# Indexer scores over four PSUM banks, and a retention chunk's two head pairs in one bank each for products, states and outputs

## The chip, the cores and the metric

The kernel runs on one core of one Trainium2 chip. The metric is the device time of one launch in microseconds (us). TensorE (PE in the profile) multiplies, VectorE (DVE), ScalarE (ACT) and GpSimd (POOL) work on its results, SyncE (SP) issues the transfers. PSUM, into which TensorE writes, has eight banks of 128 partitions by 512 floats.

## What is computed

Two decoder layers over 1024 positions of width 1024. Each layer norms the input, projects it, and runs three branches whose gated outputs are merged: retention (chunks of 128 positions with a recurrent state), a sparse attention whose indexer picks 256 keys for each query, and a gated linear attention (GLA). Cut to what the change touches:

```
def dsa_attention(q, k, v, q_idx, k_idx, w_idx, pos):        # blocks of 128 queries
        s = jnp.einsum('bqhd,bsd->bqhs', qib, k_idx_f) * (IDX_DH ** -0.5)     # 4 indexer heads
        score = jnp.einsum('bqh,bqhs->bqs', wb, jax.nn.relu(s))
        score = jnp.where(visible[None], score, -jnp.inf)
        _, sel = lax.top_k(score, topk)                                       # topk = 256
def retention(q, k, v, pos):                                  # 8 chunks of 128, 4 heads
    scores = jnp.einsum('bnihd,bnjhd->bnhij', qc, kc) * decay
    o_intra = jnp.einsum('bnhij,bnjhe->bnihe', scores, vc)
    kv = jnp.einsum('bnjhd,bnjhe->bnhde', kc * to_end[None, None, :, :, None], vc)
    state -> chunk_decay * state + kv_n
    o_cross = jnp.einsum('bnihd,bnhde->bnihe', q_dec, prev)
    return (o_intra + o_cross)
```

## The kernel before

Each layer begins with the indexer. `idx_proj` projects eight blocks of 128 positions, and `idx_scores` does blocks 2 to 7: for each piece of up to 512 keys and each of four heads TensorE makes the head's scores with two matmuls (lines 500 and 501, from a high and a low part of the keys), ScalarE takes the positive part into a buffer `tr` (line 503, three buffers), and VectorE adds it, weighted, into the block's score row `mk` (lines 506 and 509). That makes 40 heads of a piece in a layer. A head uses one PSUM bank of the tag `sc`, of which there are two.

The top-k of the sparse attention (`topk`, lines 854 and 855) works on those rows. A step is a search for the eight largest values (MAX8) and their replacement (a small load, then MATCH_REPLACE8), each over the whole row; a block takes 32 steps. Blocks 2 to 5 may run as soon as their rows stand, and they fill VectorE between its other work.

Retention follows. `ret_v` makes the values (eight groups of 24 matmuls over the shared helper lines 223 to 225, into the banks `acc`), `ret_qk` makes queries and keys of a chunk (another such group), turns them on VectorE (lines 540 to 544, the rotation; only the last of the three, line 544, gives the `acc` bank back) and transposes them. `ret_scan` does the recurrence of chunk p, one pair of heads after the other: the products of queries and keys (line 572, bank `sc`), their decay on VectorE into `at` (line 574), the carried part (line 577, bank `o`), the new state's product (line 580, bank `sc`), the state's update on VectorE (line 585), the decayed products with the values (line 590, the same bank `o`), and on ScalarE the sums of squares (line 594) and the copy out of `o` (line 595). The gate's groups (`ret_gate`, 24 matmuls a chunk; line 613 gives their bank back) and GLA's projections come next.

The eight banks have owners: `acc` 1, `tp` 2, `o` 1, `sc` 2, and two spare ones, `x` and `y`, that a table lends out. During the indexer and retention both are lent to `acc`:

```
    own = {"acc": 1, "tp": 2, "o": 1, "sc": 2}
    spare = {"x": "acc", "y": "acc"}
        extra = [e for e in sorted(spare) if spare[e] == tag]
        n = turn[tag] = (turn[tag] + 1) % (own[tag] + len(extra))
```

No order is written by hand. The program is built with a scheduler (`schedule_with_timeline_sim=True`) that sets each engine's order ahead of time; on the chip every engine then runs its list in that order and waits at each instruction for what it needs. TensorE's matmuls of `ret_v`, `ret_qk` and the gates, called the fill below, are what the scheduler puts between the small steps of scores and scan.

Of the kernel before, what the change touches and what calls it, by code (L numbers as in the profile page):

```python
# [10 lines left out]
FT = mybir.dt.float32  # L11
# [5 lines left out]
OP = mybir.AluOpType  # L17
# [56 lines left out]
def tile_trunk(ctx: ExitStack, tc: tile.TileContext, x, c, positions, ada_w, ada_b, pre_norm, post_norm,  # L74
# [17 lines left out]
    def pool(name, bufs=1, side=None):  # L92
        return tc.alloc_tile_pool(name=name, bufs=bufs, side=side, reuse_waits="tile")
# [18 lines left out]
    def otp():  # L112
        return bank("o")

    def scp():
        return bank("sc")
# [127 lines left out]
    def blk(p):  # L244
        return slice(p * 128, (p + 1) * 128)
# [206 lines left out]
    for l in range(depth):  # L452
# [40 lines left out]
        def idx_scores(i):  # L493
            w = mk[i]
            N = (i + 1) * 128
            for c0 in range(0, N, 512):
                n = min(512, N - c0)
                for h in range(4):
                    ps = scp()
                    T.matmul(ps[:, :n], qst[:, i - 2, h], ksh[:, c0:c0 + n], start=True, stop=False)  # L500
                    T.matmul(ps[:, :n], qst[:, i - 2, h], ksl[:, c0:c0 + n], start=False, stop=True)
                    r = pi_.tile([128, 512], FT, tag="tr", bufs=3, name="tr")
                    A.activation(r[:, :n], ps[:, :n], AF.Relu)
                    wh = wts[:, i, h:h + 1]
                    if h:
# [3 lines left out]
                        V.tensor_scalar(w[:, c0:c0 + n], r[:, :n], wh, None, op0=OP.mult)  # L509
            V.tensor_add(w[:, N - 128:N], w[:, N - 128:N], cau_inv)  # L510

        for p in range(NB):
            idx_proj(p)
        for i in range(2, NB):
# [50 lines left out]

        def ret_scan(p, got):
            qz, kT, qd, kd = got
            for g in range(2):
                gs = slice(g * 256, (g + 1) * 256)
                old, new = sts[g][(p + 1) % 2], sts[g][p % 2]  # L570
                sp = scp()[:, 0:256]
                T.matmul(sp, kT[:, g], qz[:, g].rearrange("p s n -> p (s n)"), start=True, stop=True)
                at = prb.tile([128, 256], FT, tag="at", bufs=2, name="at")
                V.tensor_mul(at, sp, kc[:, K_DEC + g * 256:K_DEC + (g + 1) * 256])
                op = otp()[:, 0:256]
                if p:
                    T.matmul(op, qd[:, g], old, start=True, stop=False)
                if p < NB - 1:
                    kv = scp()[:, 0:256]
                    T.matmul(kv, kd[:, 2 * g:2 * g + 2].rearrange("p h d -> p (h d)"), vo[:, p, gs],  # L580
                             start=True, stop=True)
                    for s in range(2):
                        rs = slice(s * 64, (s + 1) * 64)
                        if p:
                            V.scalar_tensor_tensor(new[rs, blk(s)], old[rs, blk(s)], kc[rs, K_CD + g:K_CD + g + 1],
                                                   kv[rs, blk(s)], op0=OP.mult, op1=OP.add)
                        else:
                            V.tensor_copy(new[rs, blk(s)], kv[rs, blk(s)])
                for s in range(2):
                    T.matmul(op[:, blk(s)], at[:, blk(s)], vo[:, p, blk(2 * g + s)], start=p == 0,  # L590
                             stop=p == 0 or s == 1)
                sq = prb.tile([128, 128], BF, tag="sq", bufs=1, name="sq")
                for s in range(2):
                    A.activation(sq, op[:, blk(s)], AF.Square, accum_out=ssq[:, p, 2 * g + s:2 * g + s + 1])
                A.copy(vo[:, p, gs], op)
            rsq(rr[:, p, :], ssq[:, p, :], 4, 4.0 / 128, 4 * EPS)

        def head_gate(pl, wg, p, o2, r2, dst):
# [28 lines left out]
        for p in range(NB):  # L627
# [2 lines left out]
                ret_scan(p - 1, held)  # L630
            held = got
        ret_scan(NB - 1, held)
        br = pool(f"brr{l}", side="right")
        brh = br.tile([128, 4, S], FR, name="brh")
        brl = br.tile([128, 4, S], FR, name="brl")
# [480 lines left out]
```

## Time and profile before

| | |
|---|---|
| median of 3 runs | 2487.65 us (2483.64 to 2490.65) |
| the profiled execution | 2489.89 us |
| its span, first to last instruction | 2488.1 us |
| PE busy | 2395.1 us, 96% of the span |
| DVE busy | 1704.3 us, 68% |
| ACT, POOL busy | 892.9 us, 915.0 us |
| indexer's first score, layer 0 and layer 1 | 101.63 us, 1316.47 us |

Busy time is the sum over an engine's instructions. The profile also tells the TensorE clock that was granted in a stretch, as a share of full speed (1.00 is 2.4 GHz, half of it 1.2 GHz), and at a wait the instruction that ended it.

### The profile page before, as it was taken

How to read it: one execution, taken by the hardware profiler on the slowest of the kernel's cores; microseconds unless marked ns; L12 is line 12 of the kernel's file. 1: busy time of each engine (PE TensorE's matmuls, PEld its weight loads, DVE VectorE, ACT ScalarE, POOL GpSimd, SP SyncE). 2: the span in 40 equal slices, each digit the busy share in tenths (PEclk: the TensorE clock that was granted, in tenths of full speed). 3: DMA queues.
4: the chain of work that ended last, by engine and by line, in shares of the span. 5: the costliest groups of instructions: out<-in, count | busy, mean ns of one | idle time of the engine just before them, and what ended most of it. 6: DMA issues, size and time to landing. Idle time of an engine off the chain costs nothing.

```text
span 2488.1 us, 38048 instructions
## 1 busy us (share of the span) xinstructions
PE 2395.1 (96%) x13680; PEld 2032.5 (82%) x13680; DVE 1704.3 (68%) x3513; ACT 892.9 (36%) x2147; POOL 915.0 (37%) x1304
## 2 busy tenths in 40 slices
PE   8898999999999999999999899999999999999998
PEld 4777788888878998887788677887898789888777
DVE  6599997348749964567567999933554899356652
ACT  4333432232321236663433234222333212566421
POOL 4324344534522352106641244443454225310350
PEclk9999999999999999999999899999999999999999
DMA  8011112224412212007620111222321221210453
GB/s 273 22 35 35 35 41 79 59 87 145 119 60 76 66 48 64 27 22 246 201 90 1 35 35 48 64 61 85 85 63 41 85 85 35 71 41 22 140 199 110
DMA packets 153115, 194.95 MB, mean 78 GB/s; under 512 B 18703, under 2 KB 109147, under 8 KB 152926
## 3 DMA queue, kind: packets, MB, share of 16 engines
q1 hardware_dynamic: 152926, 192.52, 25.4%
q8 instruction: 107, 1.75, 0.3%
q14 instruction: 82, 0.67, 0.1%
HBM read 154.71 MB, written 37.77 MB: 77 GB/s over the span
## 4 chain that ended last, share of the span: by engine, by line
PE 73%; DVE 15%; DMA 4%; issue 3%; POOL 3%; ACT 2%; SPq 0%; DVEq 0%; POOLq 0%; ACTq 0%
PE acc L223 18%; PE acc L224 18%; PE acc L225 18%; DVE mk L855 3%; PE tp L936 2%; DVE m L854 2%; DMA craw<-in_ada_w 2%; PE sc L762 2%; PE o L958 1%; PE sc L921 1%; PE o L955 1%; PE sc L922 1%; PE o L962 1%; PE sc L223 1%; PE sc L224 1%
## 5 line engine op out<-in xcount | busy, mean ns | idle before, releaser
L223 PE MATMUL acc<-whi,hTh 128*128 128x256 f32 (+1 forms) x1600 | 509.8, 319 | 15.5 <-DVE rb L544 8.0
L225 PE MATMUL acc<-whi,hTl 128*128 128x256 f32 (+1 forms) x1600 | 507.4, 317 | 0.0
L224 PE MATMUL acc<-wlo,hTh 128*128 128x256 f32 (+1 forms) x1600 | 506.9, 317 | 0.0
L177 POOL TENSOR_TENSOR wlo<-raw,whi 128x512 fp32r<-128x512 f32 x216 | 283.1, 1318 | 374.8 <-ACT whi L176 343.6
L223 PE MATMUL acc<-hTh,whi 128*128 128x512 f32 x896 | 355.4, 397 | 2.7 <-ACT mt L287 1.8
L224 PE MATMUL acc<-hTl,whi 128*128 128x512 f32 x896 | 353.3, 394 | 0.0
L225 PE MATMUL acc<-hTh,wlo 128*128 128x512 f32 x896 | 352.7, 394 | 0.0
L854 DVE MAX8 m<-mk 128x8 f32<-128x512 f32 (+5 forms) x384 | 341.7, 892 | 8.2
L223 PEld LDWEIGHTS acc<-whi,hTh 128*128 128x128 f32 x1600 | 307.1, 192 | 41.3 <-issue 11.7
L855 DVE MATCH_REPLACE8 mk<-m,mk 128x512 f32<-128x512 f32 (+5 forms) x384 | 336.6, 877 | 0.2
L225 PEld LDWEIGHTS acc<-whi,hTl 128*128 128x128 f32 x1600 | 306.8, 192 | 20.0 <-issue 2.4
L224 PEld LDWEIGHTS acc<-wlo,hTh 128*128 128x128 f32 x1600 | 307.0, 192 | 19.0 <-issue 2.2
L176 ACT CAST whi<-raw 128x512 fp32r<-128x512 f32 x216 | 133.8, 622 | 217.9 <-PE acc L224 139.0
L223 PEld LDWEIGHTS acc<-hTh,whi 128*128 128x128 f32 x896 | 169.0, 189 | 39.9 <-ACT mt L287 2.8
L225 PEld LDWEIGHTS acc<-hTh,wlo 128*128 128x128 f32 x896 | 169.0, 189 | 37.1 <-issue 2.4
L224 PEld LDWEIGHTS acc<-hTl,whi 128*128 128x128 f32 x896 | 169.1, 189 | 34.1 <-issue 1.9
L940 DVE TENSOR_TENSOR ptl<-tp,pth 128x512 fp32r<-128x512 f32 (+1 forms) x160 | 100.6, 635 | 68.6 <-ACT pth L939 59.3
L287 ACT ACTIVATE mt<-acc 128x512 f32<-128x512 f32 x96 | 57.2, 599 | 191.1 <-PE acc L225 136.3
L218 POOL TENSOR_TENSOR wlo<-raw,whi 128x512 fp32r<-128x512 f32 x56 | 76.7, 1378 | 111.2 <-ACT whi L217 110.4
L926 ACT ACTIVATE P<-P,mx 128x256 f32<-128x256 f32 (+7 forms) x128 | 99.8, 781 | 47.0 <-DVE mx L923 46.1
L939 ACT CAST pth<-tp 128x512 fp32r<-128x512 f32 (+1 forms) x160 | 85.7, 545 | 69.5 <-PE o L955 43.3
L973 POOL TENSOR_TENSOR qo<-qo,gt 128x256 f32<-128x256 f32 x32 | 23.5, 735 | 229.4 <-DVE qo L967 208.8
(411 smaller groups left out, 4858.4 us busy)
## 6 DMA issues: line engine op xcount, KB each, us to landing
raw<-in_w_in SPq DMA_DIRECT2D x224, 256.0 KB
yscr<-mu SPq DMA_DIRECT2D x64, 256.0 KB
craw<-in_ada_w SPq DMA_DIRECT2D x64, 256.0 KB
ul<-yscr SPq DMA_DIRECT2D x64, 256.0 KB
aw<-in_ada_w SPq DMA_DIRECT2D x16, 512.0 KB
xt<-in_x SPq DMA_DIRECT2D x16, 512.0 KB
mscr<-mt SPq DMA_DIRECT2D x32, 256.0 KB
ul<-mscr SPq DMA_DIRECT2D x32, 256.0 KB
```

The costliest lines, as they stand in the source:

```text
L176: A.copy(hi[:, :, :off], raw[:, :, :off])
L177: G.tensor_sub(lo[:, :, :off], raw[:, :, :off], hi[:, :, :off].bitcast(FT))
L218: G.tensor_sub(lo, raw, hi.bitcast(FT))
L223: T.matmul(ps, ah, bh, start=start, stop=False)
L224: T.matmul(ps, ah, bl, start=False, stop=False)
L225: T.matmul(ps, al, bh, start=False, stop=stop)
L287: A.activation(t, gp, AF.Tanh, scale=0.5)
L854: V.max(m8, mk[i])
L855: V.match_replace(mk[i], m8, mk[i], TAKEN)
L926: A.activation(P[:, :N], P[:, :N], AF.Exp, scale=-1.0, bias=mx[:, nch - 1:nch], accum_out=den[:, i, n * 4 + g:n * 4 + g + 1])
L939: A.copy(pth[:, :w], tp[:, :w])
L940: V.tensor_sub(ptl[:, :w], tp[:, :w], pth[:, :w].bitcast(FT))
```

## The change

For the indexer and retention the spare bank `x` is lent to `sc`, and goes back to `acc` after the last scan. Heads 0 to 2 of a piece take `sc` banks, head 3 takes the bank `o`; `tr` has four buffers. `ret_scan` does both pairs at once: both products go into one `sc` bank and are decayed by one instruction of 512 columns; both state products go into the two halves of another `sc` bank; both outputs go into one bank `o`, the second pair's matmuls after the first pair's last, and leave it by one copy of 512 columns.

```
@@ -496,10 +496,10 @@
             for c0 in range(0, N, 512):
                 n = min(512, N - c0)
                 for h in range(4):
-                    ps = scp()
+                    ps = otp() if h == 3 else scp()
                     T.matmul(ps[:, :n], qst[:, i - 2, h], ksh[:, c0:c0 + n], start=True, stop=False)
                     T.matmul(ps[:, :n], qst[:, i - 2, h], ksl[:, c0:c0 + n], start=False, stop=True)
-                    r = pi_.tile([128, 512], FT, tag="tr", bufs=3, name="tr")
+                    r = pi_.tile([128, 512], FT, tag="tr", bufs=4, name="tr")
                     A.activation(r[:, :n], ps[:, :n], AF.Relu)
                     wh = wts[:, i, h:h + 1]
                     if h:
@@ -509,6 +509,7 @@
                         V.tensor_scalar(w[:, c0:c0 + n], r[:, :n], wh, None, op0=OP.mult)
             V.tensor_add(w[:, N - 128:N], w[:, N - 128:N], cau_inv)
 
+        spare["x"] = "sc"
         for p in range(NB):
             idx_proj(p)
         for i in range(2, NB):
@@ -565,34 +566,40 @@
 
         def ret_scan(p, got):
             qz, kT, qd, kd = got
+            sp, op = scp(), otp()
+            for g in range(2):
+                T.matmul(sp[:, g * 256:(g + 1) * 256], kT[:, g], qz[:, g].rearrange("p s n -> p (s n)"),
+                         start=True, stop=True)
+            at = prb.tile([128, 512], FT, tag="at", bufs=2, name="at")
+            V.tensor_mul(at, sp, kc[:, K_DEC:K_DEC + 512])
+            kv = scp() if p < NB - 1 else None
             for g in range(2):
                 gs = slice(g * 256, (g + 1) * 256)
                 old, new = sts[g][(p + 1) % 2], sts[g][p % 2]
-                sp = scp()[:, 0:256]
-                T.matmul(sp, kT[:, g], qz[:, g].rearrange("p s n -> p (s n)"), start=True, stop=True)
-                at = prb.tile([128, 256], FT, tag="at", bufs=2, name="at")
-                V.tensor_mul(at, sp, kc[:, K_DEC + g * 256:K_DEC + (g + 1) * 256])
-                op = otp()[:, 0:256]
-                if p:
-                    T.matmul(op, qd[:, g], old, start=True, stop=False)
-                if p < NB - 1:
-                    kv = scp()[:, 0:256]
-                    T.matmul(kv, kd[:, 2 * g:2 * g + 2].rearrange("p h d -> p (h d)"), vo[:, p, gs],
+                if kv is not None:
+                    T.matmul(kv[:, gs], kd[:, 2 * g:2 * g + 2].rearrange("p h d -> p (h d)"), vo[:, p, gs],
                              start=True, stop=True)
                     for s in range(2):
-                        rs = slice(s * 64, (s + 1) * 64)
+                        rs, cs_ = slice(s * 64, (s + 1) * 64), blk(2 * g + s)
                         if p:
                             V.scalar_tensor_tensor(new[rs, blk(s)], old[rs, blk(s)], kc[rs, K_CD + g:K_CD + g + 1],
-                                                   kv[rs, blk(s)], op0=OP.mult, op1=OP.add)
+                                                   kv[rs, cs_], op0=OP.mult, op1=OP.add)
                         else:
-                            V.tensor_copy(new[rs, blk(s)], kv[rs, blk(s)])
-                for s in range(2):
-                    T.matmul(op[:, blk(s)], at[:, blk(s)], vo[:, p, blk(2 * g + s)], start=p == 0,
-                             stop=p == 0 or s == 1)
-                sq = prb.tile([128, 128], BF, tag="sq", bufs=1, name="sq")
-                for s in range(2):
-                    A.activation(sq, op[:, blk(s)], AF.Square, accum_out=ssq[:, p, 2 * g + s:2 * g + s + 1])
-                A.copy(vo[:, p, gs], op)
+                            V.tensor_copy(new[rs, blk(s)], kv[rs, cs_])
+            mm = None
+            for g in range(2):
+                with ExitStack() as es:
+                    if mm is not None:
+                        es.enter_context(tc.issue_after(mm.ins))
+                    if p:
+                        T.matmul(op[:, g * 256:(g + 1) * 256], qd[:, g], sts[g][(p + 1) % 2], start=True, stop=False)
+                    for s in range(2):
+                        mm = T.matmul(op[:, blk(2 * g + s)], at[:, blk(2 * g + s)], vo[:, p, blk(2 * g + s)],
+                                      start=p == 0, stop=p == 0 or s == 1)
+            sq = prb.tile([128, 128], BF, tag="sq", bufs=1, name="sq")
+            for h in range(4):
+                A.activation(sq, op[:, blk(h)], AF.Square, accum_out=ssq[:, p, h:h + 1])
+            A.copy(vo[:, p, :], op)
             rsq(rr[:, p, :], ssq[:, p, :], 4, 4.0 / 128, 4 * EPS)
 
         def head_gate(pl, wg, p, o2, r2, dst):
@@ -630,6 +637,7 @@
                 ret_scan(p - 1, held)
             held = got
         ret_scan(NB - 1, held)
+        spare["x"] = "acc"
         br = pool(f"brr{l}", side="right")
         brh = br.tile([128, 4, S], FR, name="brh")
         brl = br.tile([128, 4, S], FR, name="brl")
```

The scheduler sets another order with it. Three places follow, all of layer 0, as the order of each program lists them.

TensorE, around the last heads of the indexer's scores (lines 500 and 501; `sc` and `o` are the banks, `acc` rows are the fill). Before:

```order
L500 MATMUL sc<-ksh,qst 128x512
L501 MATMUL sc<-ksl,qst 128x512
L500 MATMUL sc<-ksh,qst 128x512
L501 MATMUL sc<-ksl,qst 128x512
L572 MATMUL sc<-qz_1143,kT 128x256
L580 MATMUL sc<-vo,kd 128x256
L223 MATMUL acc<-whi,hTh 128x512
```

and with the change:

```order
L500 MATMUL sc<-ksh,qst 128x512
L501 MATMUL sc<-ksl,qst 128x512
L225 MATMUL acc<-whi,hTl 128x512
L500 MATMUL sc<-ksh,qst 128x512
L501 MATMUL sc<-ksl,qst 128x512
L500 MATMUL sc<-ksh,qst 128x512
L501 MATMUL sc<-ksl,qst 128x512
L223 MATMUL acc<-whi,hTh 128x512
L500 MATMUL o<-ksh,qst 128x512
L501 MATMUL o<-ksl,qst 128x512
L224 MATMUL acc<-wlo,hTh 128x512
L225 MATMUL acc<-whi,hTl 128x512
```

Heads came in pairs with about 20 fill matmuls between pairs, and the last ten heads stood together with no fill between them, straight before retention's first products. Now they come in fours with 13 to 17 fill matmuls between, the last four are done at the fill's 166th matmul (before: after its 312th), and 98 fill matmuls follow in one run.

VectorE, where the rotation comes whose end TensorE first has to wait for (`mk_488` is block 3's row, `mk_487` block 2's; MAX and MATCH_REPLACE are a top-k step). Before, chunk 2's rotation:

```order
L854 MAX m_7633<-mk_488 128x8
L855 MATCH_REPLACE mk_488<-m_7633,mk_488 128x512
L854 MAX m_7636<-mk_488 128x8
L563 TENSOR_TENSOR qd<-tp,kc 128x256
L540 TENSOR_TENSOR ra<-acc,cs 128x512
L542 TENSOR_TENSOR rb<-acc,nsn 128x8x32
L544 TENSOR_TENSOR rb<-acc,sn 128x8x32
L574 TENSOR_TENSOR at<-sc,kc 128x256
```

and with the change, chunk 0's:

```order
L863 MATCH_REPLACE mk_488<-m_7539,mk_488 128x512
L862 MAX m_7542<-mk_488 128x8
L863 MATCH_REPLACE mk_488<-m_7542,mk_488 128x512
L862 MAX m_7545<-mk_488 128x8
L863 MATCH_REPLACE mk_488<-m_7545,mk_488 128x512
L541 TENSOR_TENSOR ra<-acc,cs 128x512
L543 TENSOR_TENSOR rb<-acc,nsn 128x8x32
L545 TENSOR_TENSOR rb<-acc,sn 128x8x32
```

Counted from the first weighted score, 93 halves of a top-k step (a MAX or a MATCH_REPLACE) stood ahead of chunk 2's rotation in layer 0 and 103 in layer 1; ahead of chunk 0's stand now 70 and 75.

TensorE, the state products of line 580 with the change (numbered names are kept here: `sc_1762` is chunk 3's bank for them, `sc_1833` chunk 4's; what stands in brackets are the engines that an instruction waits for):

```order
L580 MATMUL sc_1833<-vo_1140,kd_1748 128x256 [waits DVE_49,Pool_49]
L223 MATMUL acc_1854<-whi_1413,hTh_83 128x512
L571 MATMUL sc_1827<-qz0_1143,kT_1752 128x256 [waits DVE_49,PE_49,Activation_49]
L571 MATMUL sc_1827<-qz0_1143,kT_1752 128x256
L224 MATMUL acc_1854<-wlo_1414,hTh_83 128x512
L225 MATMUL acc_1854<-whi_1413,hTl_84 128x512
L223 MATMUL acc_1854<-whi_1419,hTh_83 128x512
L224 MATMUL acc_1854<-wlo_1420,hTh_83 128x512
L225 MATMUL acc_1854<-whi_1419,hTl_84 128x512
L580 MATMUL sc_1762<-vo_1140,kd_1677 128x256 [waits DVE_49]
```

The second pair's state product now waits for VectorE, which reads the first pair's half of the same bank. In layer 0 it comes 11 to 27 fill matmuls after the first pair's (here `sc_1762` gets its second half, 17 fill matmuls after its first). There are 14 such in the program. Outside the indexer, retention and the first stages of GLA that follow them, the order of every engine is unchanged in layer 1; in layer 0 it is also changed up to GLA's second scan.

## Rows read from the trace of the kernel before

**Rows 1.** The page's first part: an engine's busy us, share of the span, instructions.

```profile
PE 2395.1 (96%) x13680; PEld 2032.5 (82%) x13680; DVE 1704.3 (68%) x3513; ACT 892.9 (36%) x2147; POOL 915.0 (37%) x1304
```

**Rows 2.** Busy time by stretch: us; PE, PEld, DVE, ACT, POOL busy; PEclk; DMA share, GB/s.

```profile
100.00:160.00 60.00, 60.00 (x284) 49.88 (x283) 51.77 (x125) 21.83 (x46) 11.21 (x9) 1.00 0.13 36
160.00:215.00 55.00, 46.67 (x196) 35.71 (x196) 53.94 (x124) 14.82 (x38) 10.65 (x16) 0.88 0.00 1
215.00:284.00 69.00, 65.05 (x326) 54.17 (x325) 66.16 (x152) 27.36 (x94) 24.34 (x28) 1.00 0.12 31
1390.00:1440.00 50.00, 41.46 (x178) 32.40 (x177) 48.83 (x110) 14.77 (x41) 10.54 (x16) 0.86 0.01 2
1440.00:1500.00 60.00, 57.11 (x281) 46.28 (x280) 58.38 (x130) 22.32 (x82) 21.31 (x25) 1.00 0.13 34
```

**Rows 3.** PE's waits, whole run: who waited for whom, us in total, times, longest.

```profile
PE acc L223 <- DVE rb L544: 8.0, 5, 3.4
PE sc L572 <- ACT kT L559: 7.0, 2, 4.3
PE acc L223 <- ACT qT L687: 6.2, 2, 3.7
PE sc L500 <- ACT tr L503: 4.3, 9, 0.8
PE o L577 <- ACT vo L595: 4.2, 5, 1.8
```

**Rows 4.** Timeline of PE: start us, us, instruction, in brackets idle before and its releaser.

```profile
101.63 0.42 PE L500 MATMUL sc<-ksh,qst 128*128 128x384 f32 x1
...
196.97 0.76 PE L223 MATMUL acc<-whi,hTh 128*128 128x512 f32 x1 [3.42 <-DVE rb L544]
...
1316.47 0.34 PE L500 MATMUL sc<-ksh,qst 128*128 128x384 f32 x1
```

**Rows 5.** Timeline of DVE around chunk 2's rotation, layer 0.

```profile
193.04 0.68 DVE L854 MAX8 m<-mk 128x8 f32<-128x512 f32 x1
...
194.55 0.69 DVE L854 MAX8 m<-mk 128x8 f32<-128x512 f32 x1
...
195.48 0.68 DVE L540 TENSOR_TENSOR ra<-acc,cs 128x512 f32<-128x512 f32 x1
...
196.41 0.42 DVE L544 TENSOR_TENSOR rb<-acc,sn 128x256 f32<-128x256 f32 x1
196.74 0.42 DVE L574 TENSOR_TENSOR at<-sc,kc 128x256 f32<-128x256 f32 x1
```

**Rows 6.** Timeline of DVE: chunk 2's rotation of layer 1.

```profile
1417.92 0.42 DVE L544 TENSOR_TENSOR rb<-acc,sn 128x256 f32<-128x256 f32 x1
```

**Rows 7.** Timeline of PE: fill matmuls, then one chunk's scan matmuls (one instruction is x2).

```profile
93.18 0.39 PE L225 MATMUL acc<-whi,hTl 128*128 128x512 f32 x1
93.41 0.39 PE L223 MATMUL acc<-whi,hTh 128*128 128x512 f32 x1
...
221.02 0.59 PE L572 MATMUL sc<-qz,kT 128*128 128x256 f32 x2
221.45 0.59 PE L577 MATMUL o<-st,qd 128*128 128x256 f32 x2
221.88 0.61 PE L590 MATMUL o<-vo,at 128*128 128x128 f32 x4
```

**Rows 8.** Timeline of DVE: gate products and top-k steps over 640 columns, layer 0.

```profile
256.05 1.14 DVE L615 SCALAR_TENSOR_TENSOR gt<-vo,rr,gt 128x128 f32<-128x128 f32 x4
257.10 0.08 DVE L855 MATCH_VALUE_LOAD mk<-m,mk 128x8 f32 x1
...
258.02 0.83 DVE L854 MAX8 m<-mk 128x8 f32<-128x640 f32 x1
...
259.80 0.83 DVE L854 MAX8 m<-mk 128x8 f32<-128x640 f32 x1
```

**Rows 9.** Timeline of DVE: the last decay of layer 0.

```profile
280.70 0.43 DVE L574 TENSOR_TENSOR at<-sc,kc 128x256 f32<-128x256 f32 x1
```

**Rows 10.** DVE's groups, 100 to 320 us: busy us, mean ns of one, idle before.

```profile
L585 DVE SCALAR_TENSOR_TENSOR st<-st,kc,sc 64x128 f32<-64x128 f32 x24 | 8.2, 341 | 0.2
```

## The prediction

> **What bounds it now.** The page's first part comes first: PE is busy 96% of the span, DVE 68% [rows 1]. The change takes no product from PE, so only time in which PE stands, or runs at half clock, can be won, and only where the order changes: the indexer and retention of each layer. Next the busy time by stretch there [rows 2]. In layer 0 PE is full up to 160 us, busy 46.67 of 55 up to 215, and 65.05 of 69 up to 284; DVE is busy 53.94 of those 55. So for a while DVE is the late one. The granted clock of the middle stretch is 0.88 against 1.00 around it: 0.12 of 55 us lacks in a mean of two levels half a clock apart, so 0.12 x 55 x 2 = 13.2 us were run at half clock, after PE had stood. Layer 1 repeats it: 41.46 of 50 at 0.86, then 57.11 of 60.
>
> The waits of PE say for what [rows 3]: `acc` banks held by line 544 (the rotation on DVE) 8.0 us, buffers `tr` 4.3, the bank `o` held by the copy of line 595 4.2, and 7.0 for `kT`, which is made from the same rotation. The longest, 3.42 us, ends at 196.97 [rows 4], just behind the rotation of chunk 2, which ends at 196.41 + 0.42 = 196.83 [rows 5]. Ahead of that rotation DVE works through top-k steps [rows 5]. So the rotation is not slow; it stands late in DVE's list.
>
> What this loses on PE: idle (55 - 46.67) + (69 - 65.05) = 12.3 us in layer 0, (50 - 41.46) + (60 - 57.11) = 11.4 in layer 1. Half-clock time does half the work while PE is busy: 13.2 x 0.85 / 2 = 5.6, and 0.14 x 50 x 2 = 14.0, x 0.83 / 2 = 5.8. Together **35.1 us** is what there is to win.
>
> **The change part by part.**
>
> *Scores over four banks.* The same 80 matmuls a layer run in fours. DVE's weighted additions stay as many; only the turns change. The gain is in the fill: the last ten heads stood uncovered after the fill's 312th matmul, and now end at its 166th. A fourth `tr` buffer and four banks take most of the 4.3 us of `tr` waits [rows 3]; these lie inside the idle already counted, so they are not added again.
>
> *What waits next.* TensorE now reaches the first rotation-bound `acc` bank earlier, and DVE reaches the rotation earlier, as fewer top-k halves stand ahead. The new first point is chunk 0's rotation. I work both sides out from the first score, 101.63 us [rows 4].
>
> DVE, layer 0: the orders show 93 - 70 = 23 halves fewer than ahead of chunk 2's rotation. A step of 512 columns takes 194.55 - 193.04 = 1.51 us [rows 5], a half 0.755: 17.4 us. Two rotations less, at 196.74 - 195.48 = 1.26 from start to next start [rows 5]: 2.5; one multiply of `qd`, some 0.3. Sum 20.2, so the rotation ends at 196.83 - 20.2 = 176.6, 75.0 us after the first score. DVE stood 60 - 51.77 = 8.2 us in 100 to 160 [rows 2]; the new order has a block's row ready at once there, and I let 0 to 4 us of it go: 71 to 75.
>
> PE, layer 0: 216 fill matmuls precede, with scores that by columns (48 of 512, 16 of 384, 8 of 256, 8 of 128) are worth 66 more. A fill matmul takes 0.2275 us (93.18 to 93.41 [rows 7], a mean over more of them): 282 x 0.2275 = 64.2, and 20 transposes at about half a fill matmul each, an estimate, 2.2: 66.4. So **PE is 4.6 to 8.6 us early** and waits that long.
>
> DVE, layer 1: 28 halves less (103 to 75) x 0.755 = 21.1, and 2.8 as above; chunk 2's rotation ended at 1418.34 [rows 6], so chunk 0's ends at 1394.4, 78 us after the first score at 1316.47 [rows 4], or 74 to 78. PE: (240 + 66) x 0.2275 + 1.3 = 70.9. It waits 3 to 7.
>
> Second point, the last decay of layer 0, which ended at 281.13 [rows 9]. Ahead of it stand 11 steps of 640 columns less, at 259.80 - 258.02 = 1.78 [rows 8]: 19.6. Five gates' sums and three residues less, at 0.6 each (an estimate from the 0.68 of one pass over 512 columns [rows 5]), and five sets of gate products at 257.10 - 256.05 = 1.05 [rows 8]: 10.1; the merged decays 0.5. So it ends at 250.9, 149.3 us after the first score, or 145 to 149. PE: (412 + 66) x 0.2275 = 108.7; 60 transposes 6.5; 43 scan matmuls at 0.43 (221.02 to 221.45 [rows 7]) 18.5; 30 of half the width 6.5: 140.2. It is 5 to 9 us early. This is the same lag as at the first point, not a second one: DVE is behind once.
>
> *Both pairs together in the scan.* One decay of 512 columns for two of 256 and one copy out of `o` for two save DVE and ACT an instruction's start each, 8 times a layer, some 1 us, beside other work; in the sum it is in the 0.5 above. The second state product now waits until DVE has read the first half of its bank: two updates of 341 ns, 0.68 us [rows 10]. There are 14. In layer 0 11 to 27 fill matmuls lie between, 2.5 to 6.1 us, so what covers them is the fill; if that cover is gone, each costs at least 0.68, 9.5 us in all. With DVE 3 to 9 us behind, the wait falls inside the lag just counted (a PE that waits at a state product does not wait again at the next `acc` bank). I add nothing, and keep 9.5 as the upper end. The bank `o`: one copy of 512 columns must end before the next chunk's output, where the first pair's copy used to block the second; I let half of the 4.2 us stay, 2.1.
>
> *The Trainium skill, PSUM — Partial Sum Buffer, "PSUM bank collisions raise a hardware error", says that two engines may not touch one bank and the same 32 partitions at once, other columns or not. By that rule the wait between the two halves is no choice of the scheduler's, and two pairs in one bank are slower than in two; the sum by it would be the 9.5 us end, or rival C. No run here shows a collision.*
>
> *`x` lent to `sc`.* `idx_proj` and `ret_v` fill two `acc` banks in turn where they had three. A group of 24 matmuls is 24 x 0.2275 = 5.5 us; the eviction of the bank before lies under it. Taken as 0, at most 3 us. Nothing is gained by it there.
>
> **Sum.** Left as lateness: 7 us in layer 0 (the middle of 5 to 9, the later point) and 5 in layer 1 (the middle of 3 to 7): 12. Gain 35.1 - 12 = 23.1, less 2.1 = **21 us**. The profiled execution took 2489.89 us, 2.2 above the median of the runs: 2489.9 - 21 = 2468.9, or **2467** on the scale of the median, 0.8% faster. What a measurement can tell from no change is 0.3%, 7.5 us, so faster begins below 2480.2.
>
> **Rivals.**
>
> A. *All of it goes.* DVE may come to the rotations earlier than counted, since its 8.2 us of early idle could go whole, and PE then never stands or drops its clock. For it: the late points are only 3 to 9 us. Against: DVE has the same work ahead and is busy 98% of the middle stretch. Gain 35, up to 41 if the 6.2 us waits on line 687 [rows 3] shorten too: about 2451.
>
> B. *DVE stays the bound.* The fill that is now left for later hides nothing if DVE's list up to GLA is as long as before: PE's earlier arrival is then given back at the wait for line 687 (6.2 us [rows 3], one of up to 3.7 a layer), which grows. Only the direct `tr` waits of 4.3 us go, and a little clock: 2483 to 2486, no change. For it: DVE is full throughout 160 to 284 [rows 2]. Against: what fills DVE there includes top-k steps that can be done later under GLA, and the order puts fewer of them ahead.
>
> C. *Slower: the shared state bank makes PE wait for DVE.* Its place is line 580's second pair. Behind the first pair's product DVE has to come to the two updates; where two top-k halves stand before them the wait is 2 x 0.83 + 0.68 = 2.4 us [rows 8, 10], behind which the fill queues on PE. Were the fill between to be used up by DVE's lag rather than to cover it, 14 such cost 34 us, on top of the 12 and some 5 us of half clock (what a layer loses by it now): 51 against today's 35.1 and the 4.2 of the bank `o`, so 11 to 12 more: 2499. It decides from about 1.6 us each (12 + 14 x 1.6 + 5 = 39). For it: the bank must be handed over twice a chunk where two banks needed no handing over. Against: 11 to 27 fill matmuls, 2.5 to 6.1 us, stand between.
>
> **How the numbers follow.** My forecast has 0.74, A 0.10, B 0.11, C 0.05. The forecast's own bounds: lag 7.6 (4.6 + 3) to 16 (9 + 7) in place of 12, the shared bank 0 to 9.5, two `acc` banks 0 to 3, `o` 0 to 4.2. All lower ends give 35.1 - 7.6 = 27.5, 2460; the lag's upper end with the shared bank's leaves 35.1 - 16 - 2.1 - 9.5 = 7.5, 2480. To hold 8 in 10 the range reaches down toward A and a little above 2480: 2454 to 2481. Faster by over 0.3%: the forecast and A, 0.84; within 0.3%: B, 0.11; slower: C, 0.05.
>
> **What would show it.** Right: in layer 0's 100 to 290 us and layer 1's stretch after its first score, PE's idle falls from some 12 us to about 5 to 9 in each, no stretch's granted clock lies under 0.93, and the largest wait of PE there is once a layer for line 545's rotation of chunk 0 or what follows from it, 3 to 8 us. Waits for `tr` fall under 1 us. The last decay of layer 0 ends near 250 us. Line 580's waits on DVE sum to under 5 us. The waits for line 687's successor (695) stay near 6 us. Wrong: PE's wait for DVE at line 580 summing to over 15 us (C); the waits at line 695 over 15 us with the score stage's idle gone (B); no rotation wait left (A); or a changed sum of PE's busy time, which would mean that something other than waiting and clock moved.

## The result, and the profile after

The changed kernel took **2465.64 us** (median of 4 runs, 2463.37 to 2468.41); the kernel before 2488.56 us in 4 runs. The ratio is 0.9911, with a 95% interval of 0.9893 to 0.9929: 17.7 to 26.6 us faster. The forecast was 2467 us, so the total came out. It came out by luck: its terms for the changed stages were 16.9 us too careful, and what happens outside them, which it put at nothing, cost 16.4 us. Most of what follows is about these two.

The page's first part, as in [rows 1]:

```profile
PE 2388.5 (97%) x13680; PEld 2033.8 (82%) x13680; DVE 1689.7 (69%) x3497; ACT 888.9 (36%) x2131; POOL 913.8 (37%) x1304
```

Busy time by stretch, the stretches of [rows 2], columns as there (us; PE, PEld, DVE, ACT, POOL busy; PEclk; DMA share, GB/s):

```profile
100.00:160.00 60.00, 60.00 (x287) 49.98 (x286) 56.21 (x143) 29.37 (x62) 7.27 (x13) 1.00 0.05 14
160.00:215.00 55.00, 53.17 (x265) 44.83 (x264) 53.15 (x124) 15.43 (x57) 20.97 (x23) 1.00 0.09 25
215.00:284.00 69.00, 69.00 (x344) 57.48 (x343) 67.76 (x148) 27.54 (x73) 25.54 (x27) 1.00 0.17 43
1390.00:1440.00 50.00, 50.00 (x258) 42.93 (x257) 48.21 (x112) 18.73 (x68) 19.29 (x22) 1.00 0.06 14
1440.00:1500.00 60.00, 59.88 (x296) 49.49 (x295) 59.14 (x126) 22.10 (x59) 19.41 (x20) 1.00 0.17 44
```

Where PE stood 12.3 and 11.4 us, it now stands 55 - 53.17 = 1.8 in layer 0 and 0.1 in layer 1, and the granted clock is 1.00 in all five stretches: nearly all of what there was to win in the indexer and in retention is won. PE's waits over the whole run, as in [rows 3]:

```profile
PE acc L223 <- DVE ul L1060: 11.3, 12, 3.4
PE tp L254 <- POOL hht L248: 10.4, 3, 6.3
PE o L782 <- DVE ats L776: 9.1, 5, 3.3
...
PE acc L223 <- ACT qT L695: 3.9, 2, 2.8
...
PE sc L770 <- DVE st L761: 2.1, 2, 1.9
PE acc L223 <- DVE rb L545: 1.8, 1, 1.8
...
PE sc L767 <- DVE st L759: 1.6, 1, 1.6
```

The waits for `tr`, for the copy out of `o` and for `kT` are gone, that for the rotation is down from 8.0 to 1.8 us, in one piece. What has grown stands elsewhere: lines 767 to 782 are GLA's scan, where the waits for `ats` were 5.9 us before and are 9.1 now.

To see where the time came from and went, I took the start of the same matmul, by its place in PE's list of 13680, in both traces, and subtracted. Positive is earlier than before:

| matmul | its start before, us | where | the change is earlier by |
|---|---|---|---|
| 650th | 164.4 | layer 0, indexer | -2.5 |
| 1500th | 346.9 | layer 0, retention done | 16.5 |
| 2700th | 564.7 | layer 0, GLA's second scan begins | 15.6 |
| 4500th | 859.0 | layer 0, sparse attention | 4.8 |
| 7350th | 1360.4 | layer 1, indexer | 5.5 |
| 8250th | 1561.1 | layer 1, retention done | 24.4 |
| last | 2480.7 | | 21.5 |

Where the two lists differ (the changed stages of both layers, and layer 0 up to the second scan) the rows are good to about 1 us; from the 4500th on, and in layer 1 outside the stages, the lists are nearly the same. The account: -2.5 in the opening (up to 110 us the waits for `hht` of line 248 are 9.0 us where they were 7.2), **+19.0** in layer 0's stage, **-11.7** after it, +0.7, **+18.9** in layer 1's stage, -2.9 at the end, together 21.5.

10.8 of the 11.7 us go in one place, between the 2700th and the 4500th matmul. Busy time around layer 0's second GLA scan, before:

```profile
555.00:615.00 60.00, 58.40 (x473) 52.89 (x472) 45.18 (x117) 16.91 (x49) 24.79 (x33) 1.00 0.46 135
615.00:675.00 60.00, 57.72 (x475) 52.40 (x474) 45.42 (x116) 17.79 (x54) 30.12 (x42) 1.00 0.47 139
```

and with the change, where the scan begins 15 us earlier:

```profile
540.00:600.00 60.00, 53.19 (x398) 47.95 (x397) 43.13 (x105) 15.68 (x48) 27.29 (x38) 0.91 0.35 105
600.00:660.00 60.00, 57.38 (x464) 52.62 (x457) 39.18 (x100) 16.84 (x52) 25.97 (x35) 0.97 0.53 156
```

PE stands 6.81 + 2.62 = 9.4 us against 1.60 + 2.28 = 3.9 before, and at a granted clock of 0.91 and 0.97 it ran (0.09 + 0.03) x 60 x 2 = 14.4 us at half, with PE busy some 0.9 of it: 14.4 x 0.9 / 2 = 6.5 us of work lost. 5.5 + 6.5 = 12.0, about what the table shows.

Between 540 and 660 us PE waits 5.7 us for VectorE's `ats`, the masked scores of the scan, and 3.7 for its states `st`; before it was 2.9 and 1.0. Ahead of the states stand six condition sums with waits of 1.5 and 1.0 us for their loads (546.20 to 552.17 us) and a gate's sum that waits 2.2 us for ScalarE (554.55). VectorE's timeline with the change, just before PE's longest wait of 3.3 us, which ends at 588.31:

```profile
575.71 0.66 DVE L325 SCALAR_TENSOR_TENSOR ca<-craw,th,ca 128x256 f32<-128x256 f32 x1 [0.55 <-DMA craw<-in_ada_w]
576.29 0.43 DVE L771 COPY_PREDICATED ats<-km,sc 128x256 f32<-128x256 uint8 x1
576.62 0.76 DVE L325 SCALAR_TENSOR_TENSOR ca<-craw,th,ca 128x256 f32<-128x256 f32 x1
577.30 0.29 DVE L776 COPY_PREDICATED ats<-km,sc 128x128 f32<-128x128 uint8 x1
579.11 0.48 DVE L325 SCALAR_TENSOR_TENSOR ca<-craw,th,ca 128x256 f32<-128x256 f32 x1 [1.52 <-DMA craw<-in_ada_w]
579.51 0.30 DVE L776 COPY_PREDICATED ats<-km,sc 128x128 f32<-128x128 uint8 x1
...
582.51 2.74 DVE L612 SCALAR_TENSOR_TENSOR vo<-vo,grr,gt 128x128 f32<-128x128 f32 x2
585.17 1.48 DVE L325 SCALAR_TENSOR_TENSOR ca<-craw,th,ca 128x256 f32<-128x256 f32 x1
586.58 0.43 DVE L776 COPY_PREDICATED ats<-km,sc 128x128 f32<-128x128 uint8 x1
...
587.83 0.43 DVE L776 COPY_PREDICATED ats<-km,sc 128x128 f32<-128x128 uint8 x1
```

The seven `ats` copies of a step of the scan do not stand together: between them stand sums of the condition (line 325), which wait for their loads `craw`, and gate products (line 612). The condition's sums here are this layer's last part and the next layer's first two; the code hands them out between the scan's steps (`gla_scan(1, ..., between)`).

Sums stand between the copies before, too. VectorE's step there with as many of them, its first copy, its one wait for a load and its last copy:

```profile
593.61 0.44 DVE L763 COPY_PREDICATED ats<-km,sc 128x256 f32<-128x256 uint8 x1
...
597.39 0.67 DVE L325 SCALAR_TENSOR_TENSOR ca<-craw,th,ca 128x256 f32<-128x256 f32 x1 [0.22 <-DMA craw<-in_ada_w]
...
599.38 0.43 DVE L768 COPY_PREDICATED ats<-km,sc 128x128 f32<-128x128 uint8 x1
```

This step holds five sums, five other instructions and 0.2 us of waits for `craw`, and takes 599.38 + 0.43 - 593.61 = 6.2 us. The change's, from 576.29, holds five sums, ten others and 1.5 us of such waits, and takes 587.83 + 0.43 - 576.29 = 12.0. So it is not that sums stand there, but what else was put into the same step: the same work, in another order, makes PE wait.

### The profile page after: what moved, and what is told of

It is laid out like the page before. It is cut to its first block, busy times and chain, and to the rows that moved or that the text cites. A ratio compares the mean times of both kernels' runs of the same rounds, so it can differ in the third digit from the quotient of the medians.

```text
span 2466.6 us, 38037 instructions
## 1 busy us (share of the span) xinstructions
PE 2388.5 (97%) x13680; PEld 2033.8 (82%) x13680; DVE 1689.7 (69%) x3497; ACT 888.9 (36%) x2131; POOL 913.8 (37%) x1304
## 4 chain that ended last, share of the span: by engine, by line
PE 76%; DVE 13%; DMA 4%; issue 3%; POOL 3%; ACT 2%; SPq 0%; DVEq 0%; POOLq 0%; ACTq 0%
PE acc L223 18%; PE acc L224 18%; PE acc L225 18%; DVE mk L863 3%; PE tp L944 2%; DVE m L862 2%; DMA craw<-in_ada_w 2%; PE sc L770 2%; PE o L966 1%; PE sc L929 1%; PE o L963 1%; PE sc L930 1%; PE o L970 1%; DVE gt L622 1%; PE sc L223 1%
```

## The experiments

Two questions: which half of the change won the stages, and why 11.7 us went back. Each set of runs had runs of the kernel before beside it (medians 2487.80, 2486.91 and 2485.87 us), to which its ratios refer; a difference between kernels of different sets is surer by the ratios than by the medians.

For the second question there were three theories. *List*: the order that the scheduler now sets in that scan costs it. *Shift*: whoever comes 16 us earlier has to wait there for transfers that don't come earlier. *Shared loads*: the two `craw` buffers limit the scan in any case. Lists were compared row by row, without buffer numbers, from the first to the last condition sum of layer 0 on VectorE; "95 of 100 rows" is the share that agrees. Other engines' lists change along with VectorE's. The diffs are against the change unless the text says otherwise.

### Scores alone

```
+        spare["x"] = "acc"
         ret_v()
...
-            sp, op = scp(), otp()
...
+                sp = scp()[:, 0:256]
+                T.matmul(sp, kT[:, g], qz[:, g].rearrange("p s n -> p (s n)"), start=True, stop=True)
...
```

`ret_scan` is that of the kernel before, one pair after the other; `x` goes back to `acc` ahead of it.

> Scores over four banks as in the change; the scan as before, bank x back with acc before retention. Scores theory (the gain in both layers' indexer and retention comes from the scores' turns, which let the last heads end early in the fill): PE's idle in 160 to 284 us and in layer 1's stretch falls from 12 and 11 us to 1 to 5 each, 75 and 80 top-k halves stand ahead of chunk 0's rotation against 70 and 75 with the whole change, so up to 4 us a layer less of the gain; the stages give 30 to 37 us. Its VectorE list in layer 0's second GLA scan is nearly that of the change, so by either theory below some 10 to 13 us go back there: 2463 to 2473. Scan theory (the gain comes from the pairs' merging): within 6 us of before, 2482 or more.

Measured: 2466.64 us, ratio 0.9918 (0.9902 to 0.9935). By matmuls, layer 0's stage gives 10.7 + 3.9 = 14.6 us and layer 1's 20.7 - 3.3 = 17.4; 10.7 - 4.8 = 5.9 go back by the 4500th, 5.4 of them in the second GLA scan. So the scores' turns carry most of the stages' gain, 32 of 38 us. It arrives at that scan 5 us later than the change and leaves it at the same time, with nearly the same list: this alone would also fit the shift theory.

### The scan alone

```
-                    ps = otp() if h == 3 else scp()
+                    ps = scp()
-                    r = pi_.tile([128, 512], FT, tag="tr", bufs=4, name="tr")
+                    r = pi_.tile([128, 512], FT, tag="tr", bufs=3, name="tr")
-        spare["x"] = "sc"
...
-        spare["x"] = "acc"
```

> Both pairs in one bank in the scan, scores over two banks as before, no bank lent. Scores theory: the last ten heads still stand uncovered, 93 and 103 top-k halves still stand ahead of chunk 2's rotation; only the waits for the bank o (4.2 us) and some of the later ones go, so 0 to 6 us: 2482 to 2489. Scan theory: 15 us or more, 2473 or less. VectorE's list in layer 0's second GLA scan is word for word that of before, so list theory (the order there costs the 12 us) and shift theory (whoever comes 16 us earlier waits there for transfers) both let nothing be given back, since it arrives hardly earlier.

Measured: 2478.18 us, ratio 0.9958 (0.9942 to 0.9975), 9.6 us faster than the before of its runs: more than the 0 to 6 that were expected. Busy time by stretch of this kernel:

```profile
160.00:215.00 55.00, 48.00 (x199) 36.52 (x198) 52.75 (x121) 15.41 (x39) 10.98 (x16) 0.88 0.00 1
215.00:284.00 69.00, 69.00 (x352) 58.66 (x352) 67.39 (x151) 29.69 (x96) 25.45 (x30) 1.00 0.12 31
1390.00:1440.00 50.00, 42.32 (x180) 33.22 (x179) 47.18 (x106) 16.34 (x46) 11.01 (x13) 0.90 0.00 1
1440.00:1500.00 60.00, 60.00 (x308) 51.10 (x308) 58.79 (x129) 23.62 (x79) 20.65 (x25) 1.00 0.15 36
```

The uncovered heads stand as before (48.00 of 55 at 0.88; 46.67 in [rows 2]), but the later stretch of each layer, 65.05 of 69 and 57.11 of 60 before, is full. Merging the pairs wins the second part by itself; the scores alone fill the first (55.00 of 55, and 66.22 of 69 behind it). Together they give less than the sum (38 against 32 + 14); that either also shortens what the other cures would explain it and was not tried. Hardly anything went back in the second scan (4.5 earlier at the 2700th, 3.7 at the 4500th), with before's list.

### Two `tr` buffers: before's list, at the change's time

```
-                    r = pi_.tile([128, 512], FT, tag="tr", bufs=4, name="tr")
+                    r = pi_.tile([128, 512], FT, tag="tr", bufs=2, name="tr")
```

> The whole change, with two tr buffers in place of four. Its TensorE reaches GLA as early as with the change (14 to 18 us earlier than before in layer 0, less up to 4 us of waits for tr), but its VectorE list in layer 0's second GLA scan is word for word that of before. List theory: nothing is given back between 540 and 660 us; total gain 32 to 38 us, 2451 to 2457. Shift theory: 9 to 13 us are given back there as with the change, 2463 to 2468. If tr buffers matter most: over 2470, with PE waiting for line 503 for over 10 us.

Measured: **2451.11 us**, ratio 0.9854 (0.9839 to 0.9870), 14.5 us faster than the change (14.2 by the ratios). It reaches the scan 17.7 us earlier than before, earlier than the change, and leaves it 17.4 earlier: nothing goes back. The shift theory falls. Its busy time there, and then PE's waits from 540 to 660 us (who waited for whom, us, times, longest):

```profile
540.00:600.00 60.00, 57.87 (x468) 52.35 (x467) 48.14 (x123) 15.31 (x45) 24.78 (x33) 1.00 0.47 139
600.00:660.00 60.00, 57.81 (x475) 52.49 (x475) 44.85 (x116) 18.38 (x55) 32.94 (x47) 1.00 0.45 135
```

```profile
PE o L782 <- DVE ats L776: 3.3, 4, 1.1
PE sc L770 <- DVE st L761: 0.6, 1, 0.6
PE sc L767 <- DVE st L761: 0.3, 1, 0.3
```

The longest wait is 1.1 us, and the clock stays at 1.00. It also shows that the change's four `tr` buffers were not needed: with two the stages give 21.1 and 21.7 us.

### Two `tr` buffers and a bank for each pair's states: the change's list again

```
-            kv = scp() if p < NB - 1 else None
...
-                if kv is not None:
+                if p < NB - 1:
+                    kv = scp()
```

> The kernel with two tr buffers, and the two pairs' state products in a bank of their own each. Its orders of scores and rotations are those of two tr buffers in all but a half step; its VectorE list in layer 0's second GLA scan, however, is word for word that of the change, where that of the kernel with two tr buffers was that of before. List theory: the same gain in the stages, then 9 to 13 us given back between 540 and 660 us: 2461 to 2467. Without an effect of the list: 2449 to 2455 as with two tr buffers. Shared-bank theory (one bank for both pairs' states makes TensorE wait): 3 to 9 us more won in the stages than with two tr buffers; since no idle stood before line 580 with the change, 0 to 1 is expected.

Measured: 2465.15 us, ratio 0.9916 (0.9899 to 0.9932). Layer 0's stage gives 17.1 + 2.9 = 20.0 us, against 21.1 with the shared bank: sharing cost nothing. Then 16.4 earlier at the 2700th and 8.1 at the 4500th: 8.3 us go back, with the change's list, in a kernel that differs from the last one only in where two half banks lie. PE's waits from 540 to 660 us:

```profile
PE o L782 <- DVE ats L776: 4.3, 2, 2.4
PE sc L770 <- DVE st L761: 2.0, 2, 1.8
PE sc L767 <- DVE st L759: 1.9, 1, 1.9
```

They are the waits of the change (5.7, 2.1 and 1.6 us in the same stretch). That it is the order is shown by these two runs together: nearly the same stages, same time of arrival within 1.3 us, lists exchanged, and 0.3 against 8.3 us given back. From the first to the last condition sum every row of PE, VectorE, ScalarE and GpSimd stands as before in the one kernel and as in the change in the other. So which engine's order costs the time is not separated; PE's waits point to VectorE's. The profiled execution is the fastest of this kernel's four (2459.82 to 2468.92 us): the medians of the two kernels lie 14 us apart, their traces 10.

### A third buffer for the condition's loads

In the kernel with two `tr` buffers, in the change, and in the kernel before, each with this edit alone:

```
-            raw = pl.tile([128, 2, 256], FT, tag="craw", bufs=2, name="craw")
+            raw = pl.tile([128, 2, 256], FT, tag="craw", bufs=3, name="craw")
```

> The kernel with two tr buffers, with three buffers for the condition's loads (craw) instead of two. Its list in layer 0's second scan is like that of before in 82 of 100 rows. If the craw loads limit the scan even with that list: VectorE's waits for craw between 540 and 660 us (12.2 us with before's list) fall by half and 2 to 5 us are won, 2446 to 2449. If they are covered there: 2449 to 2454, as with two buffers.

> The whole change with its four tr buffers, and three buffers for the condition's loads. Its VectorE list in layer 0's second GLA scan is like neither that of before (40 of 100 rows) nor that of the change (53). If what the change's list costs are waits for craw that stand between the scan's steps: they fall from 13.4 us to under 5 between 540 and 660 us, and the 11.7 us given back become a gain of up to 5 instead: 2447 to 2455. If the places of the steps in the list cost it, not the loads: 9 to 13 us still go back, 2462 to 2468.

> The kernel before with three craw buffers and nothing else. If the third buffer's gain has nothing to do with the change: 3 to 6 us faster than before, 2481 to 2485, all of it between 540 and 660 us of layer 0; indexer and retention as before. If it is a gain only for a kernel that comes early: within 2 us of before.

Measured: with two `tr` buffers **2447.77 us**, ratio 0.9839 (0.9824 to 0.9854); the change 2451.12, ratio 0.9856 (0.9834 to 0.9878); the kernel before 2481.76, ratio 0.9986 (0.9975 to 0.9996). The kernel before gains 4.1 us by the medians; in its trace 4.2 come in the scan (0.5 earlier at the 2700th, 4.7 at the 4500th). The change gains 14.5 (13.7 by the ratios): it no longer gives 11.7 back but is 1.7 earlier at the 4500th than at the 2700th. VectorE's wait for `craw` between 540 and 660 us was this in the kernel before:

```profile
DVE ca L325 <- DMA craw<-in_ada_w: 9.3, 12, 1.5
DVE ca L327 <- DMA craw<-in_ada_w: 2.9, 3, 1.4
```

In the change it was 11.9 + 1.5 = 13.4, and with the third buffer it falls to these:

```profile
DVE ca L327 <- DMA craw<-in_ada_w: 1.5, 2, 1.3
DVE ca L325 <- DMA craw<-in_ada_w: 1.0, 2, 0.7
```

The sum of these waits is not what makes the difference, however: it was 12.2 us in the kernel before and 12.8 with two `tr` buffers, where nothing was lost. It matters how much of them falls into one step of the scan. Before's list bears the waits; that the change's list would be harmless without them is not shown. It was not run with three buffers: the scheduler then sets a third order (53 of 100 rows as with the change), in which, from 570 us on, two sums stand in a step in place of five. So the third buffer works together with the order that comes with it, and how much is due to either stays open.

> Two tr buffers and four craw buffers. With three, VectorE still waited 3.1 us for craw between 540 and 660 us and TensorE 1.1 us for VectorE. If the third buffer was enough: 2445 to 2450, as with three. If the list matters beyond the loads (here 73 of 100 rows like before, 69 like the change): 2450 to 2458.

With four buffers (and two `tr`): 2450.8 us, ratio 0.9854 (0.9836 to 0.9872). A fourth buffer is not faster than three. The median lies just inside the expectation's second case, but the intervals of the two kernels overlap, so it does not tell the cases apart.

### The condition's parts behind the scan

```
-        g1 = gla_scan(1, got1, [partial(cond_part, p1, l_, part, cg) for l_, part in conds for cg in range(4)])
+        g1 = gla_scan(1, got1)
...
+        for l_, part in conds:
+            for cg in range(4):
+                cond_part(p1, l_, part, cg)
         gla_gate(1, got1[3], g1)
```

> The whole change, with the condition parts (the sums over craw of layer 0's and the next layer's condition) written behind the second GLA scan and not between its steps. If what costs in the list are the condition's waits for craw that stand between the scan's steps on VectorE: PE's waits for lines 759, 761 and 776 between 540 and 660 us fall from 9 to under 3 us, and 8 to 12 of the 11.7 us come back: 2453 to 2459. If they only move: VectorE waits for craw later, and the gates' groups or the merge stand still: 2462 or more.

Measured: 2503.98 us, ratio 1.0068 (1.0052 to 1.0084): slower than before, the expectation's second case. But it holds both halves of the answer. Through the scan the kernel *gains*: 16.5 earlier at the 2700th matmul, 25.3 at the 3600th. Then it stands behind it, where nothing is left to cover the loads:

```profile
PE tp L329 <- DVE ca L325: 53.1, 8, 7.1
```

So the condition's sums do cost the scan (it takes 8.8 us less than before when they are gone), and yet the scan is the cover that they need.

### No bank lent, and the bank lent longer

```
-        spare["x"] = "sc"
...
-        spare["x"] = "acc"
```

> The whole change but x stays with acc: scores over two sc banks and o, the scan with two sc banks. The heads come in threes and end later in the fill (254th matmul after the first score, before 312th and with the change 142nd), 82 top-k halves ahead of chunk 2's rotation. If three banks are enough to cover the heads: stages give 30 to 38 us as with the change. If the fourth bank is what counts: PE keeps 6 to 10 us of idle a layer, the stages give 12 to 20 us. Its list in layer 0's second GLA scan is like that of the change in 77 of 100 rows, so list theory allows 0 to 13 us given back there: 2452 to 2470 in the first case, 2468 to 2482 in the second.

Measured: 2459.53 us, ratio 0.9890 (0.9872 to 0.9908). The stages give 12.3 and 18.1 us, the lower end of the expectation's first case; three banks cover all of layer 1 and leave 55 - 50.60 = 4.4 us of idle in layer 0. (The expectation's 312th matmul is counted from another start; from the first score it is the 274th.) Only 4.2 us go back from the 1500th to the 4500th matmul, and the opening is 1.4 us earlier than before where the change's is 2.5 later. So lending `x` wins some 7 us in layer 0's stage; the change loses them again behind it, and 4 more ahead of it.

> The whole change with its four tr buffers; x goes back to acc only after GLA's first scan instead of after retention's last. Orders up to retention's end as with the change; the VectorE list in layer 0's second GLA scan is like that of before in 95 of 100 rows. List theory: 0 to 3 us given back between 540 and 660 us, so 2449 to 2458, if two acc banks in place of three cost GLA's first projections nothing; at worst 5 us more. Without an effect of the list: 10 to 13 given back, 2462 to 2470.

The edit moves `spare["x"] = "acc"` from the end of retention to the end of GLA's first scan. Measured: 2577.18 us, ratio 1.0367 (1.0347 to 1.0386), a miss in every case that was written down. From the 1500th to the 2400th matmul 58.7 us are lost, and some 55 more in layer 1. PE waits for VectorE in GLA's first scan:

```profile
PE o L781 <- DVE ats L775: 69.5, 17, 11.7
```

VectorE is in the midst of top-k steps over 768 columns then, placed between the `ats` copies. That GLA's groups had two `acc` banks in place of three is the edit; how the scheduler came from there to this order was not tried. As a test of the list theory it says little: with before's list it gives back 0.8 us in the second scan, but it comes there 49 us late.

## Why the prediction was right, and where it was not

- **What bounds the kernel, and what there was to win (35.1 us).** Right. The stages gave 19.0 + 18.9 = 37.9; the 2.3 us by which the waits for line 695 became shorter (6.2 to 3.9) are in it and were not in the 35.1. A changed sum of PE's busy time was named as a sign of something else at work. The sum fell from 2395.1 to 2388.5 us, but the sign was badly chosen: at half clock the same work counts as busy for longer (a fill matmul takes 0.76 us behind the wait at 196.97 [rows 4] and 0.39 in [rows 7]). Of such time 5.6 + 5.8 us went in the stages and 6.5 came in the scan.
- **What is late next: the rotation of chunk 0.** The place was right, the size not. It was put at 4.6 to 8.6 us in layer 0 and 3 to 7 in layer 1; measured are 1.8 and none. Of the two sides PE's was good, VectorE's was too late. PE, with the change:

```profile
100.84 0.42 PE L500 MATMUL sc<-ksh,qst 128*128 128x384 f32 x1
...
170.25 0.47 PE L223 MATMUL acc<-whi,hTh 128*128 128x512 f32 x1 [1.82 <-DVE rb L545]
...
1312.70 0.34 PE L500 MATMUL sc<-ksh,qst 128*128 128x384 f32 x1
```

and VectorE:

```profile
169.69 0.41 DVE L545 TENSOR_TENSOR rb<-acc,sn 128x256 f32<-128x256 f32 x1
...
242.55 0.69 DVE L574 TENSOR_TENSOR at<-sc,kc 128x512 f32<-128x512 f32 x1
...
1382.69 0.69 DVE L541 TENSOR_TENSOR ra<-acc,cs 128x512 f32<-128x512 f32 x1 [1.31 <-PE acc L225]
1383.30 0.41 DVE L543 TENSOR_TENSOR rb<-acc,nsn 128x256 f32<-128x256 f32 x1
1383.63 0.41 DVE L545 TENSOR_TENSOR rb<-acc,sn 128x256 f32<-128x256 f32 x1
```

  PE came to the point 170.25 - 1.82 - 100.84 = 67.6 us after the first score (66.4 were worked out). The rotation ended 170.10 - 100.84 = 69.3 after it, not 71 to 75. In layer 1 it ended at 71.3, not 74 to 78, and there it is VectorE that waits for PE, 1.31 us. The last decay of layer 0 ended at 142.4, not 145 to 149. What was mis-sized is the allowance "I let 0 to 4 us of it go": VectorE's idle time between 100 and 160 us fell from 8.2 to 60 - 56.21 = 3.8 us, so 4.4 went, just past the whole allowance where I had used its middle; the rest, some 1.3 us, is in the count. **Rival A** was nearly the right one for the stages.
- **The shared bank of the states.** Taken as 0, and it was: no idle time stands before line 580, and a bank for each pair won nothing. Rival C falls. The Trainium skill's rule (PSUM — Partial Sum Buffer, "PSUM bank collisions raise a hardware error") says that two engines may not touch one bank and the same 32 partitions at once. By that rule the second product has to wait for VectorE's reads; the wait is there in the order, and 11 to 27 fill matmuls cover it. A collision itself no run here shows.
- **The bank `o`, 2.1 us kept.** The wait for its copy is gone altogether: 2.1 us too careful.
- **`x` lent to `sc`.** Taken as 0, at most 3 us; it goes with the 2.5 us that the opening lost. PE's busy time in the first 100 us, before and with the change:

```profile
0.00:100.00 100.00, 81.27 (x345) 58.95 (x346) 58.45 (x104) 38.19 (x74) 53.23 (x86) 0.90 0.55 183
0.00:100.00 100.00, 78.39 (x334) 57.17 (x335) 59.30 (x104) 37.39 (x73) 52.54 (x84) 0.90 0.55 183
```

  In the nine kernels that lend `x` to `sc` during the indexer it is 78.4 to 79.8 us, in the four that do not 81.3 to 82.7. Whether the bank that `acc` lacks or the order that comes with it costs this was not separated.
- **Rival B** (PE's gain given back at the wait for line 695) falls: that wait became shorter.
- **The term that was missing.** The sum ended with retention. That the order is also changed up to GLA's second scan stood in the section on the change, and it was priced at nothing without naming what covers it. It cost 11.7 us. VectorE's condition sums and their two buffers stood there in the trace of before, with 12.2 us of waits for loads.
- **The total.** The stages gave 37.9 us where 21 were forecast, 16.9 more: of the 12 kept as lateness less than 2 were left, the 2.1 for `o` was not needed, and line 695 gave 2.3. That makes some 14.5; the rest stays open. Against this stand 11.7 lost behind layer 0's stage, 2.5 in the opening and 2.9 at the end, less 0.7: 16.4. That 21 were forecast and the traces show 21.5 is therefore luck. Of the signs that the prediction named, the clock at 1.00 and the waits for `tr` and at line 580 came as forecast. The idle time of 5 to 9 us, a rotation wait in both layers, a last decay near 250 us (it ended at 243.2) and waits for line 695 near 6 us did not.

The fastest version run is the change with two `tr` buffers and three `craw` buffers, 2447.77 us: 17.9 us faster than the change, 1.6% faster than before. Its interval overlaps that of two `tr` buffers with two `craw` buffers (0.9839 to 0.9870), so the last 3 us are not clear of noise; in the traces the scan wins 4.5 us with it and loses 0.3 without.

## What to carry to other kernels

Where a scheduler sets the order, a change in one stage can reorder another that it does not touch: price every stretch whose order differs, not only the one that was edited, and look in it for steps with a wait of their own that now stand between the steps that the busiest engine waits for. When two kernels differ in such an order, find a third that has the one's stages and the other's order; here a buffer count did that. And where an order only happens to bear a wait, try a further buffer: in none of the four kernels with three or four `craw` buffers was anything lost in the scan.

## What was not expected of the hardware

VectorE's line 612, two instructions of 128 columns, takes 0.61 us a pair (574.56), but 2.74 at 582.51, and line 325 then 1.48 where it takes 0.48. GpSimd at that moment, with the change:

```profile
582.52 3.85 POOL L177 TENSOR_TENSOR wlo<-raw,whi 128x512 fp32r<-128x512 f32 x3
```

Three instructions of GpSimd, 3.85 us, run beside three of VectorE that take 2.74 + 1.48 = 4.2 us and would take some 1.1. The Trainium skill, SBUF — State Buffer, "SBUF: two separate sides", says that a VectorE instruction with two inputs in SBUF and one of GpSimd that reads SBUF take a port pair in turn, each for its whole length; these rows agree with that: three instructions of the one beside three of the other. It adds some 3 us to the step in which PE's longest wait arose. Lengthened sums stand in the kernel before as well (five of line 325 take 1.27 to 1.54 us between 560 and 670 us), and in the kernel with two `tr` buffers, which gives nothing back (seven, 1.18 to 1.47): it matters where they fall. No run took GpSimd's work away from there, so how much of the 11.7 us hangs on it stays open.
